# An encoder trunk on one core: the sample's laid-out x and one padded convolution row go to four buffers of their own

## The chip, the cores and the metric

The kernel runs on one core of a Trainium2 chip. The metric is device time in microseconds of one execution; each figure for the whole kernel is the median of several runs. All times inside the kernel are counted from the start of the span of one profiled execution.

The engines are called by their short names: PE (TensorE, matmuls), DVE (VectorE), ACT (ScalarE), POOL (GpSimd) and SP (SyncE, which here issues all DMAs). Each engine works through its own instructions strictly in order; an instruction that has to wait holds up all behind it on that engine.

## The reference

Two independent requests, a prompt of 512 tokens and a sample of 1024 tokens, go through one layer with the same weights (width 1024):

```
h = RMSNorm(x);  z = h @ w_in          # columns: q 512, k 128, v 128, ca 512, cb 512
A = windowed attention(q, k, v)         # 8 heads of 64, |q-k| <= 128, bias, sink
c = ca * sigmoid(cb)
B = silu(LayerNorm(depthwise_conv31(c)))
x = x + concat(A, B) @ w_out
u = depthwise_conv3(RMSNorm(x) @ w_up)
x = x + (silu(u[:, :2816]) * u[:, 2816:]) @ w_down
y = RMSNorm(x)
```

All is float32. A product is made of three matmuls: each operand is split into a rounded part "hi" and a remainder "lo", and hi*hi, hi*lo and lo*hi are summed.

## The kernel before, in words

**Stages.** The change concerns the first stage, the projection h @ w_in. The prompt's columns are made first, then the sample's, with the prompt's attention woven in. Channels lie on the partitions and 512 tokens along a row; the prompt is one such half (nt = 0), the sample two (nt = 1, 2).

**Weight chunks.** w_in is taken in chunks of 128 columns. `chunk_raw` (L222 to L225) loads one, 512 KB; `split` (L227 to L234) makes hi with an ACT copy (L230) and lo with a POOL subtraction (L231). Each of the three tiles is 4 KB a partition. `proj` (L347 to L350) then issues 24 matmuls for one chunk and one half.

**The order of the chunks** for the prompt is cb, ca of convolution rows 0, 1, 2, then k, v, then q 0 to 3, then cb, ca of row 3. `evac` brings each result out of PSUM. For "ca" it makes a padded convolution row (L427): 512 + 30 columns for the prompt, 1024 + 30 for the sample, with zeros at both ends by two POOL memsets (L428, L429) and the middle by DVE (L432). For "q" it makes hi and lo (L436, L437) and stores them in DRAM (L441, `qsd`), from where the attention loads them in another layout (L636).

**The convolution** (`conv_items`): 25 multiply-adds of DVE into one PSUM bank behind a first multiply (L398, L402), five further taps by ACT and POOL (L391, L394, L395) for the prompt, a sum (L410), and a store to DRAM (L412).

**The sample's h** (`make_h1`, `landed`). For each half, the host's transposed copy of x is loaded in four pieces of 4 KB a partition (`load_xT`, L496: the "laid-out x"). Four matmuls (L513) spread 1/rms over a PSUM bank; DVE scales each piece (L520, two for each piece), ACT rounds (L522), and DVE and POOL in turn subtract (L523). The next piece is loaded when the one ahead is taken up.

**Buffers.** `Slots.tile` hands out named buffers from free lists: of those that are large enough the smallest size, and of these the one free for longest. There are 15 "q" (4096 bytes a partition), 4 "c" (4224), 61 "h" (2048) and 2 "d" (2176). An optional `among` limits the choice to some kinds. A buffer that is handed out again brings a wait: its first writer waits for the last reader of what lay in it. So before the change the laid-out x and the weight chunks (raw, hi, lo) share the 15 "q"; the four "c" serve only the sample's four padded rows; the prompt's four padded rows lie in d0, d1, a "q" and d0 again.

**What sets the order.** In this stage a list scheduler with its own cost model lays out each engine's instructions when the program is built; with other buffers it finds other waits and makes another order. The same priorities and the same instructions go in. From the second feed-forward pass on, PE's order is written by hand.

**Names.** In the order below, a tile is named by its kind and two running numbers (b_39 is a PSUM bank's 39th use); where the buffer is shown, its number stands behind the letter (q7 is the eighth "q"). Bank uses: a_34, a_35, a_36, u_37 are the prompt's q 0 to 3; b_39 and b_40 are cb and ca of row 3; b_41 and b_48 are the sample's first chunk; u_42, a_43, a_44, a_45 are scores of the first attention unit and u_46 the first of the second unit. `h_169`, `h_174`, `h_179`, `h_185` are the lo tiles of q 0 to 3, `q_209` holds q as loaded for the first two units.

## Time and profile before

| | |
|---|---|
| median of 3 runs | 1494.17 us (1493.98 to 1497.1) |
| span of the profiled execution | 1495.0 us, 0.8 above that median; no other time of this execution is shown |
| PE busy | 1474.9 us, 99% of the span |
| DVE busy | 1142.9 us, 76% |
| ACT busy | 799.9 us, 54% |
| POOL busy | 676.3 us, 45% |
| mean granted PE clock | 0.997 of full speed |

A row of the timeline gives start, duration, engine, line, operation, output and inputs, and in brackets how long the engine had been idle and who released it. Matmuls overlap: a row of 0.39 us is followed by the next after 0.23 us. A row of the waits gives who waited for whom, the sum, the number of times and the longest. A row of the windows gives, for a stretch, the busy time of each engine, the granted PE clock, the busy share of the DMA engines and the GB/s.

### The profile page before, as it was taken

Reading aid. Unit: us, or ns where it says so; the run is one execution under the profiler, and the core shown is the slowest. Engines: PE = TensorE matmul, PEld = TensorE weight load, DVE = VectorE, ACT = ScalarE, POOL = GpSimd, SP = SyncE. Lnnn points to the kernel's source line nnn. Section 1 sums busy time; section 2 is a strip of 40 time slices with the busy share of each in tenths; the row PEclk is TensorE's granted clock in tenths of the full one; section 3 lists DMA queues with packets and bytes.
Section 4 is the critical chain, followed back from the end, with each engine's and each line's share of the span. In section 5 each row is a group of like instructions: output and inputs, shape, how many; then the busy total and the mean of one; then the engine's idle time right before and its main releaser. Section 6 shows DMA issues by size and latency. Waiting matters only on the chain.

```text
span 1495.0 us, 19855 instructions
## 1 busy us (share of the span) xinstructions
PE 1474.9 (99%) x6808; PEld 1222.4 (82%) x6808; DVE 1142.9 (76%) x1616; ACT 799.9 (54%) x1417; POOL 676.3 (45%) x540
## 2 busy tenths in 40 slices
PE   9989999999999999999999999999999999999998
PEld 7878888887888888778888888888887888888886
DVE  4999998778689876856868777777776855568884
ACT  7635665336777776444355555544444633434354
POOL 6842444235656565744325555555544000003345
PEclk9999999999999999999999999999999999999999
DMA  8862346274433346784213333333332772356644
GB/s 281 278 198 81 99 122 198 86 220 137 133 113 117 123 130 218 239 284 165 85 57 107 106 106 104 100 102 102 101 114 79 226 266 85 109 173 226 216 167 169
DMA packets 221761, 225.08 MB, mean 151 GB/s; under 512 B 12331, under 2 KB 161843, under 8 KB 221532
## 3 DMA queue, kind: packets, MB, share of 16 engines
q1 hardware_dynamic: 221660, 223.82, 46.5%
q8 instruction: 53, 0.87, 0.2%
q14 instruction: 48, 0.39, 0.1%
HBM read 164.77 MB, written 60.05 MB: 150 GB/s over the span
## 4 chain that ended last, share of the span: by engine, by line
PE 51%; DMA 3%; DVE 2%; POOL 2%; issue 1%; ACT 1%; SPq 0%; POOLq 0%; DVEq 0%; ACTq 0%
PE w L1227 9%; PE w L1228 9%; PE w L1229 9%; PE w L1578 7%; PE w L1577 7%; PE w L1579 7%; DMA c<-gt 2%; DMA gb<-c 1%; PE u L838 1%; PE u L840 1%; PE u L839 1%; DVE h L231 1%; DVE q L1090 0%; PE c L838 0%; PE c L839 0%
## 5 line engine op out<-in xcount | busy, mean ns | idle before, releaser
L231 POOL TENSOR_TENSOR q<-q,q 128x1024 fp32r<-128x1024 f32 x71 | 172.0, 2429 | 95.9 <-ACT q L230 28.2
L1090 POOL TENSOR_TENSOR q<-q,q 128x512 fp32r<-128x512 f32 x101 | 142.8, 1421 | 149.2 <-ACT q L1213 138.3
L1090 DVE TENSOR_TENSOR h<-h,h 128x512 fp32r<-128x512 f32 (+2 forms) x202 | 156.7, 809 | 64.9 <-ACT h L1094 27.3
L1579 PE MATMUL w<-h,h 128*128 128x512 f32 x462 | 179.7, 389 | 0.0
L1577 PE MATMUL w<-h,h 128*128 128x512 f32 x458 | 178.2, 389 | 0.0
L1578 PE MATMUL w<-h,h 128*128 128x512 f32 x458 | 178.2, 389 | 0.0
L1227 PE MATMUL w<-h,q 128*128 128x512 f32 x448 | 174.9, 390 | 1.4 <-ACT w L1310 1.1
L1229 PE MATMUL w<-h,q 128*128 128x512 f32 x448 | 174.3, 389 | 0.0
L1228 PE MATMUL w<-h,q 128*128 128x512 f32 x426 | 165.8, 389 | 0.0
L347 PE MATMUL u<-h,q 128*128 128x512 f32 x368 | 146.7, 399 | 2.5 <-DVE h L967 2.5
L348 PE MATMUL u<-h,q 128*128 128x512 f32 x368 | 144.4, 392 | 0.0
L350 PE MATMUL u<-h,q 128*128 128x512 f32 x360 | 141.4, 393 | 0.3
L402 DVE SCALAR_TENSOR_TENSOR c<-c,cvw,c 128x512 f32<-128x512 f32 x184 | 138.1, 751 | 2.5
L1087 POOL TENSOR_TENSOR q<-q,q 128x1024 f32<-128x1024 f32 x12 | 32.3, 2706 | 229.7 <-DMA h<-gb 190.0
L1094 ACT CAST h<-h 128x512 fp32r<-128x512 f32 x120 | 72.2, 622 | 97.6 <-DVE h L1090 41.5
L347 PE MATMUL b<-h,q 128*128 128x512 f32 x264 | 105.6, 400 | 4.8 <-ACT q L230 4.8
L348 PE MATMUL b<-h,q 128*128 128x512 f32 x264 | 104.3, 395 | 0.0
L350 PE MATMUL b<-h,q 128*128 128x512 f32 x264 | 103.9, 395 | 0.0
L1579 PEld LDWEIGHTS w<-h,h 128*128 128x128 f32 x462 | 86.7, 188 | 18.0
L1577 PEld LDWEIGHTS w<-h,h 128*128 128x128 f32 x458 | 86.0, 188 | 18.0
L1578 PEld LDWEIGHTS w<-h,h 128*128 128x128 f32 x458 | 86.0, 188 | 17.7
L1227 PEld LDWEIGHTS w<-h,q 128*128 128x128 f32 x448 | 84.1, 188 | 19.6 <-ACT w L1310 1.5
(447 smaller groups left out, 3649.9 us busy)
## 6 DMA issues: line engine op xcount, KB each, us to landing
q<-in_w_up SPq DMA_DIRECT2D x88, 512.0 KB, 4.4
ga<-q SPq DMA_DIRECT2D x64, 256.0 KB, 2.0
h<-ga SPq DMA_DIRECT2D x57, 256.0 KB, 3.3
q<-in_w_in SPq DMA_DIRECT2D x28, 512.0 KB, 4.6
h<-in_w_down SPq DMA_DIRECT2D x52, 256.0 KB, 3.5
q<-in_x_sample SPq DMA_DIRECT2D x15, 512.0 KB, 7.0
x1d<-q SPq DMA_DIRECT2D x11, 512.0 KB, 2.6
gt<-h SPq DMA_DIRECT2D x22, 256.0 KB, 2.4
```

The costliest lines, as they stand in the source:

```text
L231: ins = (nc.vector if dve else nc.gpsimd).tensor_tensor(lo[:], raw[:], hi[:].bitcast(F32), op=ALU.subtract)
L347: nc.tensor.matmul(out, whi[:, kc, :], hi[:], start=(kc == 0), stop=False)
L348: nc.tensor.matmul(out, whi[:, kc, :], lo[:], start=False, stop=False)
L350: nc.tensor.matmul(out, wlo[:, kc, :], hi[:], start=False, stop=(kc == KC - 1))
L402: nc.vector.scalar_tensor_tensor(acc[:], src(t), w(t), acc[:], op0=ALU.mult, op1=ALU.add)
L1090: (eng or nc.vector).tensor_tensor(out, a, b, op=ALU.subtract)
L1227: nc.tensor.matmul(out, whi[:, s], hi[:], start=(start and c == 0), stop=False, **go)
L1228: nc.tensor.matmul(out, whi[:, s], lo[:], start=False, stop=False, **go)
L1229: nc.tensor.matmul(out, wlo[:, s], hi[:], start=False, stop=(stop and c == 3), **go)
L1577: nc.tensor.matmul(out, sh[:, c], th[:], start=(p == 0), stop=False)
L1578: nc.tensor.matmul(out, sh[:, c], tl[:], start=False, stop=False)
L1579: nc.tensor.matmul(out, sl[:, c], th[:], start=False, stop=(p == NPAIR - 1))
```

## The change

Two buffers are chosen differently. The laid-out x (L495) takes a "c" buffer always. The padded row number 3 (L427) takes a "c" buffer; for the sample it did already, since nothing else is large enough, so this concerns the prompt's.

```diff
@@ evac, "ca", n == 0
-                cp = sb.tile([T + 2 * PAD])
+                cp = sb.tile([T + 2 * PAD], among="c" if c == 3 else None)
@@ load_xT
-            t = xT[nt, k] = sb.tile([2, NT])
+            t = xT[nt, k] = sb.tile([2, NT], among="c")
```

Eight pieces of x and five padded rows now go through the four "c" buffers, one behind another, and the 15 "q" are left to weight chunks, the rows of x for the norm, and smaller tiles. No instruction is added or removed. The orders move up to about the sample's convolutions. Three places follow.

**POOL, around the last subtraction of the laid-out x** (L523 is that subtraction, L231 the lo part of a chunk). Before:

```order
L231 TENSOR_TENSOR q10_156_845<-q1_136_763,q5_155_844 128x1024
L523 TENSOR_TENSOR h23_167_896<-q11_158_860,h57_166_895 128x512
L428 MEMSET d0_197_1138 128x15
L429 MEMSET d0_197_1138 128x15
L523 TENSOR_TENSOR h25_162_869<-q7_146_810,h54_161_868 128x512
L231 TENSOR_TENSOR q3_188_1055<-q1_180_1004,q4_187_1054 128x1024
L231 TENSOR_TENSOR q11_182_1007<-q9_175_959,q7_181_1006 128x1024
```

and with the change:

```order
L231 TENSOR_TENSOR q6_182_1007<-q10_175_959,q11_181_1006 128x1024
L231 TENSOR_TENSOR q13_188_1055<-q12_180_1004,q14_187_1054 128x1024
L523 TENSOR_TENSOR h21_144_797<-c0_135_756,h24_143_796 128x512
L231 TENSOR_TENSOR q2_195_1103<-q4_186_1052,q3_194_1102 128x1024
L523 TENSOR_TENSOR h34_153_839<-c1_139_777,h28_152_838 128x512
L523 TENSOR_TENSOR h25_162_869<-c2_146_810,h54_161_868 128x512
L523 TENSOR_TENSOR h23_167_896<-c3_158_860,h57_166_895 128x512
L231 TENSOR_TENSOR q10_208_1174<-q0_193_1100,q1_207_1173 128x1024
L428 MEMSET c0_197_1138 128x15
```

Before, the hi part of chunk 181 is written into q7, from which the subtraction h25_162 reads a piece of x; now it is written into q11, and the pieces lie in c0 to c3. The two last chunks of the prompt (181, 187) are split ahead of these subtractions, no longer behind.

**DVE, up to the lo part of the prompt's last q** (h_185, L437). Before:

```order
L402 SCALAR_TENSOR_TENSOR c_30_716<-d_76_518,cvw,c_30_716 128x512 x10
L437 SCALAR_TENSOR_TENSOR h_174_951<-a_35_921,h_173_950 128x512
L402 SCALAR_TENSOR_TENSOR c_30_716<-d_76_518,cvw,c_30_716 128x512
L437 SCALAR_TENSOR_TENSOR h_179_995<-a_36_965,h_178_994 128x512
L402 SCALAR_TENSOR_TENSOR c_30_716<-d_76_518,cvw,c_30_716 128x512
L437 SCALAR_TENSOR_TENSOR h_185_1043<-u_37_1010,h_184_1042 128x512
```

and with the change:

```order
L437 SCALAR_TENSOR_TENSOR h_169_906<-a_34_848,h_168_905 128x512
L402 SCALAR_TENSOR_TENSOR c_30_716<-d_76_518,cvw,c_30_716 128x512
L471 TENSOR_TENSOR h_150_830<-b_33_825,h_150_830 128x4x64
L523 TENSOR_TENSOR h_141_781<-c_135_756,h_140_780 128x512
L437 SCALAR_TENSOR_TENSOR h_174_951<-a_35_921,h_173_950 128x512
L523 TENSOR_TENSOR h_148_814<-c_139_777,h_147_813 128x512
L523 TENSOR_TENSOR h_160_864<-c_146_810,h_159_863 128x512
L523 TENSOR_TENSOR h_165_884<-c_158_860,h_164_883 128x512
L402 SCALAR_TENSOR_TENSOR c_30_716<-d_76_518,cvw,c_30_716 128x512
L471 TENSOR_TENSOR h_151_833<-b_33_825,h_151_833 128x4x64
L437 SCALAR_TENSOR_TENSOR h_179_995<-a_36_965,h_178_994 128x512
L437 SCALAR_TENSOR_TENSOR h_185_1043<-u_37_1010,h_184_1042 128x512
```

Fourteen L402 of the second convolution (c_30) now stand ahead of this piece, so 16 of them come before h_185 where it was 12; the 25 of the first (c_23) come before it in both. The second half's work on the laid-out x (L520, L523) now stands right in front of the lo parts of q; before it stood ahead of the second convolution.

**PE, around the first scores** (L672). Before, the first unit's scores stand within the sample's first chunk, b_41:

```order
L347 MATMUL b_41_1177<-h_105_638,q_194_1102 128x512
L348 MATMUL b_41_1177<-h_106_639,q_194_1102 128x512
L672 MATMUL u_42_1196<-h_128_735,q_209_1191 128x256
L672 MATMUL u_42_1196<-h_129_736,q_209_1191 128x256
L672 MATMUL a_43_1201<-h_128_735,q_209_1191 128x256
L672 MATMUL a_43_1201<-h_129_736,q_209_1191 128x256
L350 MATMUL b_41_1177<-h_105_638,q_195_1103 128x512
```

and with the change right behind b_39, ahead of all of b_41:

```order
L348 MATMUL b_39_1058<-h_38_291,q_181_1006 128x512
L350 MATMUL b_39_1058<-h_37_290,q_182_1007 128x512
L672 MATMUL u_42_1196<-h_128_735,q_209_1191 128x256
L672 MATMUL u_42_1196<-h_129_736,q_209_1191 128x256
L672 MATMUL a_43_1201<-h_128_735,q_209_1191 128x256
L672 MATMUL a_43_1201<-h_129_736,q_209_1191 128x256
L672 MATMUL a_44_1212<-h_128_735,q_209_1191 128x256
```

Before, 17 matmuls of b_41 precede u_42 and all 24 precede u_46; now none do, and they follow. Also, b_40 now comes as a whole ahead of b_39, and before b_39 came first by two matmuls.

## The prediction

> **What bounds the kernel now.** I read the page first. PE is busy for 99% of the span, so only its waits can be won, and they are listed by the view of waits for PE.

> ```profile
> span 1495.0 us, 19855 instructions
> PE 1474.9 (99%) x6808; PEld 1222.4 (82%) x6808; DVE 1142.9 (76%) x1616; ACT 799.9 (54%) x1417; POOL 676.3 (45%) x540
> PE b L347 <- ACT q L230: 4.8, 1, 4.8
> ```

> The longest wait is the one that touches this change: PE waits once for the hi part of a weight chunk. The timelines of PE, ACT, POOL and SP at that place show why.

> ```profile
> 83.03 0.39 PE L350 MATMUL a<-h,q 128*128 128x512 f32 x1
> 83.72 0.39 PE L350 MATMUL a<-h,q 128*128 128x512 f32 x1
> 88.94 0.80 PE L347 MATMUL b<-h,q 128*128 128x512 f32 x1 [4.84 <-ACT q L230]
> 92.44 0.40 PE L347 MATMUL b<-h,q 128*128 128x512 f32 x1
> 84.46 1.05 ACT L230 CAST q<-q 128x1024 fp32r<-128x1024 f32 x1 [5.10 <-DMA q<-in_w_in]
> 87.84 1.99 ACT L230 CAST q<-q 128x1024 fp32r<-128x1024 f32 x2 [2.34 <-POOL h L523]
> 86.54 1.27 POOL L523 TENSOR_TENSOR h<-q,h 128x512 fp32r<-128x512 f32 x1 [4.84 <-DMA cvd<-h]
> 82.24 0.34 SPq L412 DMA_DIRECT2D cvd<-h  x1
> 90.00:92.00 2.00, 2.00 (x6) 1.61 (x5) 1.97 (x4) 1.75 (x3) 2.00 (x2) 0.50 0.15 39
> ```

> PE stops after 83.72 and goes on at 88.94, when the second cast of ACT ends. That cast (chunk 181) writes q7, which L523 on POOL reads until 87.8; and this L523 waited 4.84 us for the store of the first convolution, which was issued at 82.24 and whose source it overwrites. Behind the wait PE runs at half the granted clock (0.50): from 88.94 to 92.44 are eight steps in 3.50 us. At full clock three steps take 83.72 - 83.03 = 0.69, so 0.23 each and 1.82 for eight. The stall costs 4.84 + 1.68 = **6.5 us**.

> But PE is not alone at its limit here. Grouped by shape from 25 to 95 us, and in the timeline, DVE shows:

> ```profile
> 45.00:60.00 15.00, 15.00 (x72) 12.57 (x71) 14.89 (x17) 11.80 (x21) 14.68 (x15) 1.00 1.05 362
> 60.00:75.00 15.00, 14.90 (x68) 12.01 (x67) 14.93 (x16) 7.83 (x13) 11.66 (x7) 1.00 0.53 141
> L402 DVE SCALAR_TENSOR_TENSOR c<-d,cvw,c 128x512 f32<-128x512 f32 x39 | 29.3, 752 | 0.8
> L523 DVE TENSOR_TENSOR h<-q,h 128x512 fp32r<-128x512 f32 x8 | 16.1, 2026 | 0.0
> L447 DVE TENSOR_TENSOR h<-u,h 128x512 fp32r<-128x512 f32 x1 | 0.7, 684 | 0.0
> 25.75 0.17 DVE L578 COPY vecs<-c 128x12 f32<-128x12 f32 x1 [7.22 <-PE c L570]
> 32.19 0.68 DVE L595 COPY h<-c 8x512 f32<-8x512 f32 x1 [4.70 <-PE c L593]
> 93.47 0.69 DVE L437 SCALAR_TENSOR_TENSOR h<-u,h 128x512 fp32r<-128x512 f32 x1
> ```

> In the windows the fourth number with a count is DVE's: 14.89 and 14.93 of 15 us. From 25.75 to the end of h_185 (93.47 + 0.69 = 94.16) DVE idles 4.70 us before L595 and twice 0.2, and works for 68.4 - 5.1 = 63.3 us. The eight L523 take 2.03 us each, although a subtraction of the same size takes 0.68 (L447): they meet POOL's work.

> **The change, part by part.** *The removed wait.* Chunk 181's hi now goes to q11, the last readers of which do not include an L523, and its cast stands far ahead. So the wait of 4.84 us and its half-clock phase go: -6.5. L523 of POOL may still wait for a convolution's store, but nothing of PE stands behind it.

> *The first half's x.* Its four loads move ahead of the chunk loads: 4 x 512 KB. DMA has room for them soon after: the stretch

> ```profile
> 28.00:33.00 5.00, 5.00 (x21) 3.18 (x20) 0.78 (x2) 5.00 (x8) 5.00 (x3) 1.00 0.22 71
> 33.00:45.00 12.00, 12.00 (x56) 9.90 (x55) 11.42 (x17) 6.31 (x12) 11.68 (x11) 1.00 0.97 344
> ```

> has DMA at 0.22, and at the 344 GB/s of the next row 2.1 MB take 6.1 us. Chunk loads come that much later, but the first of them is wanted by PE only behind the whole of b_24, at about 32.7. I charge nothing; without that cover the price is one load's 1.5 us. DVE fills its 4.70 us of idle time with the eight L520.

> *POOL's early order.* Between the first L395 (27.9) and the lo part of chunk 81 now stand 4 L395, 3 L231 and 3 L523. By the groups of POOL

> ```profile
> L231 POOL TENSOR_TENSOR q<-q,q 128x1024 fp32r<-128x1024 f32 x14 | 34.2, 2464 | 0.7 <-ACT q L230 0.7
> L523 POOL TENSOR_TENSOR h<-q,h 128x512 fp32r<-128x512 f32 x8 | 12.2, 1520 | 7.5 <-DMA cvd<-h 4.8 <-ACT h L522 2.7
> L395 POOL TENSOR_TENSOR h<-h,h 128x512 f32<-128x512 f32 x8 | 10.8, 1350 | 0.2
> ```

> that is 5.4 + 7.4 + 4.6 = 17.4, so 45.3. PE, with two more matmuls in front, wants it at 44.4: a new wait of 0.9 us. It costs nothing as long as PE waits longer for DVE later (next part); alone it costs the 0.9.

> *DVE's order, the step that decides.* The idle time is filled, but four more L402 come before h_185 (41, not 37): 25.75 + 63.3 + 4 x 0.75 = **92.1**, only 2.1 us earlier than 94.2. Behind h_185 hang its store, the load of q_209 for the second unit, and u_46. Before, this ran:

> ```profile
> 90.36 6.61 SPq L441 DMA_DIRECT2D qsd<-h  x10
> 99.36 0.58 SPq L636 DMA_DIRECT2D q<-qsd  x1
> 100.04 0.84 SPq L621 DMA_DIRECT2D h<-bbd  x2
> 100.93 0.90 SPq L636 DMA_DIRECT2D q<-qsd  x2
> DMA to landing us min/median/max: 5.1/5.1/5.1
> DMA to landing us min/median/max: 2.8/2.8/2.8
> 105.38 0.40 PE L672 MATMUL u<-h,q 128*128 128x256 f32 x2
> 107.94 0.40 PE L672 MATMUL u<-h,q 128*128 128x256 f32 x2
> ```

> The two landing times are of the load at 100.93 and of a lone one at 135. With the change: SP takes 0.66 us a store and issues those of h_179 and h_185 from 91.5 to 94.1, then two L621 (0.42 each), the first unit's q_209 at 95.0 and, when the last store has landed (2.4 us, as the stores of the two other stretches), the second unit's at 96.5. Two chunk loads of 512 KB no longer stand between, so the landing lies between 2.8 and 5.1; I take the middle, 4.0. First scores at 99.0, u_46 at **100.5**.

> PE is there earlier. It now runs through 83.95, needs b_40 (24 x 0.23 = 5.5) and is ready for b_39 at 89.5; b_39's bank is freed by the L471 two L437 before the end of h_185, at 90.7: wait 1.2. b_39 ends at 96.2; wait 2.8 for the first scores; these take 1.0; wait 0.5. Sum of new waits **4.5**, and by the row

> ```profile
> 658.96 0.79 PE L839 MATMUL u<-h,h 128*128 128x512 f32 x1 [2.00 <-DVE h L231]
> 659.00:662.00 3.00, 3.00 (x7) 2.42 (x8) 2.52 (x4) 1.19 (x2) 1.02 (x2) 0.50 0.82 337
> 349.00:352.00 3.00, 3.00 (x14) 2.45 (x14) 2.90 (x6) 1.72 (x3) 3.00 (x3) 1.00 0.41 121
> 348.52 0.47 PE L347 MATMUL u<-h,q 128*128 128x512 f32 x1 [1.55 <-DVE h L967]
> ```

> a wait of 2.00 us brought half clock, one of 1.55 us not. With 3.3 us of 4.3 idle I expect the half clock; part of it falls on the short score matmuls, so I charge 1.2 of the 1.68. Sum: -6.5 + 4.5 + 1.2 = -0.8, rounded down to **-0.7 us**. As a check, from the other side: u_46 and then b_41 end at 100.5 + 0.2 + 5.5 = 106.2, with 1.2 at 107.4; before, the same work ended at 108.2.

> [...]

> *Later parts.* The sample's last padded row (c0) now waits for the last read of the prompt's fourth convolution. Its memset on POOL has an L707 and an L231 behind it; before, POOL idled 7.45 us and 4.70 us near there, which covers a few us.

> ```profile
> 166.42 2.41 POOL L231 TENSOR_TENSOR q<-q,q 128x1024 fp32r<-128x1024 f32 x1 [4.70 <-ACT s L699]
> 181.21 2.39 POOL L231 TENSOR_TENSOR q<-q,q 128x1024 fp32r<-128x1024 f32 x1 [7.45 <-ACT q L230]
> ```

> **The rivals.** *One: the full gain.* If the L523 no longer meet POOL's work as often, DVE gets ahead of PE. It needs 4.5 us, 0.56 for each of the eight: a mean of 1.47 instead of 2.03. At 0.68 it would be 10.8. For it: POOL's work is split up otherwise. Against: POOL is as full as before in both stretches, and the second four L523 of DVE now stand beside four L523 and two L231 of POOL. Time 1494.2 - 6.5 = 1487.7, or 1488.6 with the early wait of 0.9.

> *Two: slower.* The same term the other way. PE now has nothing in front of u_42 and u_46, where before 24 matmuls (5.5 us) covered the way over DRAM. If h_185 ends later than about 93, each further us is paid in full. At the longest L523 that the trace has,

> ```profile
> L523 DVE TENSOR_TENSOR h<-q,h x8: 1290/2001/2820, 44.8 to 75.7; 128x512 fp32r<-128x512 f32 x8
> ```

> 2.82 for all eight, the end comes 6.4 later: 1494.2 + 5.7 = 1499.9; at 2.5, 1497.3. For it: the order is a scheduler's, which put u_42 there for data that it believed to be ready. Against: the mean was 2.03 with POOL just as busy.

> *Three: no half clock.* The idle time comes as three waits with work between them, of which the first and the last (1.2 and 0.5) are shorter than the 1.55 us at 348.52, behind which the clock stayed at 1.00; only the middle one (2.8) is longer than the 2.00 at 658.96. If the work between them keeps the clock up, 1.2 us fall away: 1492.3. Against it is the row at 659, where PE had work on both sides too. [...]

> *Four: nothing moves at the wait,* because another late reader holds the buffer of chunk 181: 1494. Against it is the order, in which the cast stands ahead.

> **How the numbers follow.** Measured against its own execution the change brings -0.7 to a span of 1495.0; the median is 0.8 below that span, so I take 1494.2 - 0.7 = **1493.5**. Chances: forecast 0.47, full gain 0.24, slower 0.16, no half clock 0.10, nothing 0.03. A landing of 2.8 or 5.1 moves the forecast by 1.2, to 1492.3 or 1494.6. The range of 8 in 10 reaches towards both sides: down to 1488.0 (between the two times of the full gain, about half of which it leaves out) and up to 1497.0 (L523 at nearly 2.5). About 0.2% (3.0 us) is what a measurement can tell from no change. Faster by more is nearly all of the full gain and a little of the third rival, 0.25; slower by more 0.15 of the 0.16; the rest, 0.60, within.

> **What would show it.** Right: no PE wait for L230 at 84 us; L437 of h_185 ending at 91 to 93; PE waiting for DVE at b_39 and for a load at L672, 3 to 6 us in all, and half clock behind it; eight L523 of about 2.0 us. Wrong: L523 means near 1.4 or 2.6, no wait at L672, or new waits of PE between 110 and 350 us, where there are none now up to 348.5.

## The result and the profile after

The changed kernel took 1498.94 us (median of 15 runs, 1495.48 to 1504.42) against 1495.33 us of the kernel before (15 runs): ratio **1.0020, 95% interval 1.0010 to 1.0029**. The ratio on record is not that of the two medians, which lie 3.6 us apart; by the ratio the change is 3.0 us slower (1.5 to 4.3), where 0.7 us faster was forecast. The predicted range ended at 1497.0. In every run an execution's time is its span plus 1.8 us, so the execution whose span of 1495.0 the prediction started from had taken 1496.8 us, 1.5 above the median of all runs of before, and not 0.8.

PE's waits in the changed kernel, from the view of waits, and the same places in PE's timeline (the row at 95.89 is the last matmul of b_39):

```profile
span 1498.9 us, 19853 instructions
PE u L672 <- DMA q<-qsd: 3.4, 1, 3.4
PE u L672 <- DVE s L679: 1.9, 1, 1.9
PE a L350 <- POOL q L231: 1.4, 1, 1.4
46.08 0.50 PE L350 MATMUL a<-h,q 128*128 128x512 f32 x1 [1.37 <-POOL q L231]
95.89 0.39 PE L350 MATMUL b<-h,q 128*128 128x512 f32 x1
99.68 0.50 PE L672 MATMUL u<-h,q 128*128 128x256 f32 x2 [3.41 <-DMA q<-qsd]
102.81 0.77 PE L672 MATMUL u<-h,q 128*128 128x256 f32 x2 [1.91 <-DVE s L679]
```

The wait of 4.84 us at 84 us is gone. In its place are 1.37 us at 46, then, behind the last matmul of b_39, 3.41 us in front of the first score (u_42) and 1.91 us in front of the second unit's (u_46): 6.7 us instead of 4.8. The windows of this stretch show the half clock behind them; the number in front of the DMA share is the granted clock.

```profile
100.00:102.00 2.00, 0.90 (x8) 0.69 (x6) 0.05 (x1) 0.00 (x0) 0.00 (x0) 0.77 0.83 221
102.00:104.00 2.00, 1.19 (x4) 1.12 (x5) 2.00 (x8) 1.21 (x5) 0.00 (x0) 0.50 0.98 367
...
106.00:108.00 2.00, 2.00 (x6) 1.58 (x5) 1.61 (x3) 0.57 (x1) 1.28 (x1) 0.52 0.01 4
```

A window of 2 us at 0.77 holds 2 x 0.23 / 0.5 = 0.92 us of half clock, one at 0.52 holds 1.92; with the two full ones between, the phase lasts 6.84 us, twice the 3.4 of before. By PE's busy time in each window it costs 2.8 us, where before it was 1.4.

Why the scores waited stands in the timelines of DVE, ACT, POOL and SP, in a group of DVE from 25 to 95 us, in SP's own waits, and in the list of DMA issues from 93 to 105 us:

```profile
60.85 0.69 DVE L447 TENSOR_TENSOR h<-u,h 128x512 fp32r<-128x512 f32 x1 [2.12 <-ACT h L446]
89.80 0.68 DVE L437 SCALAR_TENSOR_TENSOR h<-u,h 128x512 fp32r<-128x512 f32 x1
L523 DVE TENSOR_TENSOR h<-c,h 128x512 fp32r<-128x512 f32 x8 | 11.5, 1462 | 0.0
92.17 1.95 ACT L394 ACTIVATE h<-q,cvw 128x512 f32<-128x512 f32 x3 [6.14 <-DMA qsd<-h]
92.97 2.68 POOL L395 TENSOR_TENSOR h<-h,h 128x512 f32<-128x512 f32 x2 [2.05 <-ACT h L394]
94.31 1.72 SPq L621 DMA_DIRECT2D h<-bbd  x2
96.11 0.38 SPq L636 DMA_DIRECT2D q<-qsd  x1
97.06 0.38 SPq L636 DMA_DIRECT2D q<-qsd  x1
SPq L621 <- POOL h L395: 2.3, 2, 1.4
q<-qsd SPq DMA_DIRECT2D x3, 256.0 KB, 5.7
```

DVE was not late: h_185 ended at 90.48. But on SP two loads of the bias (L621) stand in front of the first load of q. Their buffers are those of two taps of the convolution (h55 and h26 in the order), so each waits for the L395 that reads the tap; the first L395 waits for L394 on ACT, and that one for the stores of q, in whose buffers the taps are written. So the first load of q went out at 96.11, the second at 97.06. The first score followed the first load by 3.5 us. The second unit's score came at 102.81, which is the second load's issue plus 5.7, the median landing of these loads: 102.8. The row names L679, the last thing that DVE had finished; but u_46 reads nothing of L679, and its bank (u0) was last read by the L437 that ended at 90.48. In two more profiles of this order the sum fits as well (below).

### The profile page after: what moved, and what is told of

The parts are those of the page before. It is cut to its first block, busy times and chain, and to the rows that moved or that the text cites. A ratio compares the mean times of both kernels' runs of the same rounds, so it can differ in the third digit from the quotient of the medians.

```text
span 1498.9 us, 19853 instructions
## 1 busy us (share of the span) xinstructions
PE 1477.1 (99%) x6808; PEld 1223.7 (82%) x6808; DVE 1136.3 (76%) x1616; ACT 796.7 (53%) x1417; POOL 676.1 (45%) x540
## 4 chain that ended last, share of the span: by engine, by line
PE 91%; DMA 3%; DVE 2%; POOL 1%; ACT 1%; issue 1%; SPq 0%; POOLq 0%; DVEq 0%; ACTq 0%
PE w L1227 9%; PE w L1228 9%; PE w L1229 9%; PE w L1578 7%; PE w L1579 7%; PE w L1577 7%; PE u L347 5%; PE u L348 5%; PE u L350 5%; PE b L348 3%; PE b L350 3%; PE b L347 3%; PE u L839 2%; PE u L838 2%; PE u L840 2%; PE a L672 1%
## 5 line engine op out<-in xcount | busy, mean ns | idle before, releaser
L231 POOL TENSOR_TENSOR q<-q,q 128x1024 fp32r<-128x1024 f32 x71 | 172.2, 2428 | 95.5 <-ACT q L230 23.1
L1227 PE MATMUL w<-h,q 128*128 128x512 f32 x448 | 174.9, 390 | 1.1 <-ACT w L1310 0.8
L402 DVE SCALAR_TENSOR_TENSOR c<-c,cvw,c 128x512 f32<-128x512 f32 x209 | 156.8, 750 | 2.9
L347 PE MATMUL u<-h,q 128*128 128x512 f32 x368 | 147.1, 400 | 2.8 <-DVE h L967 2.8
L350 PE MATMUL u<-h,q 128*128 128x512 f32 x360 | 141.9, 394 | 0.1
L347 PE MATMUL b<-h,q 128*128 128x512 f32 x264 | 105.5, 400 | 0.0
L350 PE MATMUL b<-h,q 128*128 128x512 f32 x264 | 104.4, 395 | 0.0
L1227 PEld LDWEIGHTS w<-h,q 128*128 128x128 f32 x448 | 84.1, 188 | 19.4 <-ACT w L1310 1.2
```

The lines of the kernel that those rows point to most:

```text
L231: ins = (nc.vector if dve else nc.gpsimd).tensor_tensor(lo[:], raw[:], hi[:].bitcast(F32), op=ALU.subtract)
L347: nc.tensor.matmul(out, whi[:, kc, :], hi[:], start=(kc == 0), stop=False)
L350: nc.tensor.matmul(out, wlo[:, kc, :], hi[:], start=False, stop=(kc == KC - 1))
L402: nc.vector.scalar_tensor_tensor(acc[:], src(t), w(t), acc[:], op0=ALU.mult, op1=ALU.add)
L1227: nc.tensor.matmul(out, whi[:, s], hi[:], start=(start and c == 0), stop=False, **go)
```

## Experiments

Each kernel was timed beside before, in one series of runs. The table gives, for the one profiled execution of each, PE's waits and its loss by half clock (sum over windows of 2 us of PE's busy time times one minus the clock) from 20 to 130 us and from 330 us to the first L1227, and the time of that instruction, all in us. Behind them stand, over all runs, the median, the median of before in the same series, and the ratio on record with its interval.

| kernel | 20 to 130: waits, half | 330 on: waits, half | first L1227 | median | before | ratio |
|---|---|---|---|---|---|---|
| before | 4.8, 1.4 | 4.8, 1.5 | 729.37 | | | |
| the change | 6.7, 2.8 | 4.6, 3.3 | 733.41 | 1498.94 | 1495.33 | 1.0020 (1.0010 to 1.0029) |
| the change again | 6.8, 4.0 | 4.0, 1.5 | 732.44 | 1499.15 | 1497.13 | 1.0016 (1.0005 to 1.0028) |
| x only | 5.6, 3.1 | 4.7, 0.0 | 730.04 | 1499.48 | 1495.47 | 1.0022 (1.0013 to 1.0031) |
| row only | 3.7, 2.8 | 5.1, 1.6 | 729.81 | 1497.17 | 1495.47 | 1.0004 (0.9993 to 1.0015) |
| scores behind | 3.2, 0.0 | 5.8, 1.7 | 728.04 | 1495.45 | 1495.47 | 1.0001 (0.9988 to 1.0013) |
| q first | 2.8, 0.0 | 5.4, 0.0 | 725.43 | 1496.27 | 1495.47 | 1.0002 (0.9992 to 1.0012) |
| first half's x | 4.5, 1.5 | 4.3, 0.0 | 727.05 | 1494.75 | 1496.14 | 0.9991 (0.9981 to 1.0001) |
| second half's x | 4.4, 0.0 | 4.8, 0.0 | 727.52 | 1495.64 | 1496.14 | 0.9992 (0.9983 to 1.0001) |
| q first, scores behind | 2.8, 0.0 | 6.2, 0.0 | 727.49 | 1495.13 | 1496.14 | 0.9993 (0.9983 to 1.0002) |
| bias early, scores behind | 16.1, 2.3 | 4.6, 0.0 | 741.33 | 1508.45 | 1496.14 | 1.0072 (1.0059 to 1.0084) |
| lo first | 3.8, 1.6 | 4.2, 1.7 | 727.48 | 1496.05 | 1497.13 | 0.9999 (0.9987 to 1.0011) |
| q and lo first | 3.1, 0.0 | 5.0, 1.7 | 726.13 | 1494.98 | 1497.13 | 0.9993 (0.9981 to 1.0005) |
| all three | 2.0, 0.0 | 5.1, 1.5 | 725.94 | 1493.13 | 1497.13 | **0.9980 (0.9968 to 0.9991)** |

From 130 to 330 us no kernel waits more than 0.9 us. The first L1227 less these four columns is 716.0 to 718.5 in every row: waits and half clock account for the differences to within 2.5 us.

The expectations were written when I still read the second wait as one for L679; where they say so, the load of q stands behind it.

### Which half of the change brings it

Only the x (the row as before), and only the row (the x as before):

```diff
-                cp = sb.tile([T + 2 * PAD], among="c" if c == 3 else None)
+                cp = sb.tile([T + 2 * PAD])
```
```diff
-            t = xT[nt, k] = sb.tile([2, NT], among="c")
+            t = xT[nt, k] = sb.tile([2, NT])
```

> Only the laid-out x takes c buffers; the prompt's fourth padded row stays where it was. Theory A (the loss comes from the first scores, which stand in front of the sample's first chunk b_41 with nothing to cover their loads; that order already comes with x alone): the old wait of 4.84 us at 84 us is gone, PE waits about 3.4 us for the load of q_209 and about 1.9 us for L679 near 96 to 103 us, and the time is 2 to 4 us above before. Rival D (the padded row, whose memsets and readers now stand in line in the c buffers, brings the loss): without the row the gain of the removed wait shows, 4 to 6 us below before.

> Only the prompt's fourth padded row takes a c buffer; the laid-out x stays among the q buffers. Theory A: the order on PE stays that of before (17 matmuls of b_41 ahead of the first scores), the wait of 4.84 us at 84 us stays, the time is that of before within 1.5 us. Rival D (the row brings the loss): 3 us or more above before, with new PE waits that before does not have.

PE's timeline with x only, then with the row only:

```profile
99.24 0.51 PE L672 MATMUL u<-h,q 128*128 128x256 f32 x2 [2.68 <-DMA q<-qsd]
102.03 0.77 PE L672 MATMUL u<-h,q 128*128 128x256 f32 x2 [1.58 <-DVE s L679]
```
```profile
87.94 0.79 PE L347 MATMUL b<-h,q 128*128 128x512 f32 x1 [3.72 <-ACT q L230]
```

x alone gives the change's order on PE and SP, its two waits and its loss; the row alone leaves the old wait and no difference that can be told. The loss is x's, and rival D is out. (With x only the second load went out at 97.22; plus its 4.7 that is 101.9, and the score came at 102.03.)

### What the place of the scores costs, and what the queue

The scores of the first four units are held behind the projection matmul that was written last before them:

```diff
+            if not late_lo:
+                ended["mm"] = ins.ins
...
-                nc.tensor.matmul(sc[:, :nk], ...)
+                with (tc.issue_after(ended["mm"]) if u < 4 and L == 0 else nullcontext()):
+                    nc.tensor.matmul(sc[:, :nk], ...)
```

or the loads of q are written ahead of those of the bias (the first ones then take h buffers):

```diff
-    load_bias()
 ...
+    load_q(0)
+    load_q(1)
+    load_bias()
```

> The change as it is, but the matmuls of the first four attention units (L672) may not be placed ahead of the projection matmul that stood last in the program when they were written: 12 matmuls of b_41 come before the first score, 24 before the second unit's. All loads, buffers and the order of the queue stay the same. Theory A (missing cover on PE makes the loss): PE reaches the first score at about 98.8 us instead of 96.05, waits at most 1 us for q_209 and not at all at the second unit, and stays at full clock: 4.4 us of waits and about 2.3 us of half clock less than the change, so about 3.5 us below before (1490 to 1493 for a before of 1495.3). Rival C (the loss lies in later parts, where the DVE or the convolutions have become late, and the waits at 96 to 103 us are only where it shows): the waits come back behind b_41 or later, and the time stays within 1.5 us of the change, 2 to 4 us above before.

> The change as it is, but in the program the loads of q for the first two units stand ahead of the eight loads of the bias (L621), so the queue has one bias load in front of them and not two or three, and they take other buffers. PE's order keeps the first scores ahead of b_41. Theory A, with the queue as what sets the length of the waits: the first score starts about 1.3 us earlier (98.4 us instead of 99.7), and the bias of the first head is there earlier, so that the wait of 1.9 us for L679 goes nearly; about 3 us below the change, that is the time of before within 1.5 us. Rival B (the lo parts of q on DVE and their stores set the start of the scores, as the prediction had it): the first score does not start earlier than 99.2 us and the time stays that of the change, 2 to 4 us above before.

PE with the scores behind, in which the lines have moved by two or three (L425 is L423, L730 is L727, L708 is L705); then SP, PE and DVE with q first (L634 is L636, L674 is L672, L681 is L679):

```profile
97.41 0.50 PE L347 MATMUL b<-h,q 128*128 128x512 f32 x1 [0.69 <-ACT h L425]
115.38 0.33 PE L730 MATMUL a<-ident,q 128*128 128x128 f32 x1 [1.19 <-ACT q L708]
```
```profile
94.85 1.32 SPq L634 DMA_DIRECT2D h<-qsd  x3
97.76 0.48 PE L674 MATMUL u<-h,h 128*128 128x256 f32 x2 [1.20 <-DMA h<-qsd]
98.79 0.40 PE L674 MATMUL u<-h,h 128*128 128x256 f32 x2
99.14 0.47 DVE L681 CUSTOM_DVE_ANT_0 q<-u,h,nsink 128x256 f32<-128x256 f32 x1
346.99 0.47 PE L347 MATMUL u<-h,q 128*128 128x512 f32 x1 [3.02 <-DVE h L969]
```

Each alone takes the loss back to before, so the two together made it: scores with nothing in front of them, and loads of q behind loads of the bias. Rival B, by which the first score would not start ahead of 99.2 us, is out (97.76). With the scores behind, b_41 runs from 97.41, where in the change it stood behind the waiting scores until 103.38, and the waits at the scores are gone; those that stay are for the bank of b_41, which tanh (L423) reads, and for the exponentials. With q first the three loads go out together at 94.85, the first score starts 1.9 us earlier than in the change and the second unit's (98.79) does not wait at all. It runs before the first L679 begins (99.14): so u_46 does not need L679, and its wait in the change was one for the load.

Theory A expected the scores-behind kernel at 1490 to 1493; it came at 1495.45. The stretch up to 130 us gave what was expected (9.5 us of waits and half clock in the change, 3.2 now), but only about half of it is in the time (ratios of 1.0020 and 1.0001: some 2.8 us, each known to between 1.5 and 2). One place where it goes back shows with q first: PE comes to the L967 wait at 346.99 - 3.02 = 343.97, 3.0 us earlier than before (348.52 - 1.55 = 346.97), and DVE releases it only 1.5 us earlier.

### Half of x

Only the first half's pieces, or only the second half's, in c (`among="c" if nt == 1 else None`, and `nt == 2`; the row as before).

> Only the first half's four pieces of x take c buffers; the second half's and the padded row stay as before the change. The list scheduler then puts the first scores still further forward: ahead of 22 matmuls of b_39 and of all of b_41. Theory A (the place of the scores on PE against the arrival of q sets the loss): PE comes to the first score some 5 us earlier than in the change and waits that much longer, 6 to 9 us in all, so the time is 4 us or more above the change (1503 or more). Rival E (the loss is that of eight pieces and five rows queueing for four buffers, which is half as much here): no slower than the change, 1495 to 1499.

> Only the second half's four pieces of x take c buffers. The old wait goes (the cast of chunk 181 waits for no L523), and the scheduler leaves 12 matmuls of b_41 in front of the first score and 24 in front of the second unit's. Theory A: without the uncovered loads the gain of the removed wait stays: no PE wait for L230 at 84 us, none above 1 us at the first scores, 3 to 6 us below before (1489 to 1492 for a before of 1495.3). Rival C (whatever is gained at 84 us is given back in later waits, since the sample's attention and convolutions are late by DVE and POOL): within 1.5 us of before, with new waits between 105 and 260 us.

SP and PE with the first half's; then PE with the second half's:

```profile
88.64 0.47 SPq L636 DMA_DIRECT2D q<-qsd  x1
84.50 0.71 PE L350 MATMUL a<-h,q 128*128 128x512 f32 x1 [2.42 <-POOL q L231]
96.65 0.40 PE L672 MATMUL u<-h,q 128*128 128x256 f32 x2
```
```profile
91.77 0.50 PE L350 MATMUL b<-h,q 128*128 128x512 f32 x1 [0.98 <-POOL q L231]
99.05 0.50 PE L347 MATMUL b<-h,q 128*128 128x512 f32 x1 [2.00 <-ACT h L423]
```

The first of these is a clear miss of theory A as I had put it. The scores stand ahead of b_39, and yet the first one does not wait: in this order the first load of q stands ahead of all bias loads, and went out at 88.64. The place on PE is not a loss by itself; only against the load's place in the queue. The second half's x alone keeps 12 matmuls of b_41 in front of the scores and has no half clock, but new waits of 0.98 and 2.00 us; it gives little.

### Both edits together, and the bias early

> The change with both edits of the two runs before: q's loads ahead of the bias loads in the program, and the first four units' scores kept behind the projection matmuls that stand ahead of them in the program. Theory A: no wait of PE at the first scores at all; what the run with the scores behind still had (0.7 us for L423 and 1.2 us for the exponentials) stays or shrinks; PE stands 5 us or more ahead of before at 250 us, and the time is 2 to 5 us below before. Rival C: the two do not add up, the time stays within 1.5 us of before like each alone, and the profile shows which later wait takes the gain.

> The change with the scores kept behind as above, and with the eight bias tiles loaded four chunks earlier in the program, so that no bias load stands in front of the first loads of q and no softmax (L679) waits for one. Theory A: no wait of PE for q or for L679 near 96 to 103 us, 2 to 5 us below before. Rival F (the bias tiles then hold buffers, one q, one d and six h, that the prompt's weight chunks and lo parts want, so new waits come before 96 us): a new PE wait between 60 and 96 us, and the time at or above that of before.

The second of these loads the eight bias tiles four chunks earlier, in the loop over the prompt's chunks:

```diff
     for i in range(npr):
+        if i == npr - 4:
+            load_bias()
```

PE with both edits (L972 is L967 there, L844 is L839); then ACT and PE with the bias early (L438 is L436, L425 is L423):

```profile
347.69 0.47 PE L347 MATMUL u<-h,q 128*128 128x512 f32 x1 [2.47 <-DVE h L972]
658.26 0.50 PE L844 MATMUL u<-h,h 128*128 128x512 f32 x1 [2.63 <-DVE h L231]
```
```profile
102.94 0.60 ACT L438 ACTIVATE h<-u 128x512 fp32r<-128x512 f32 x1 [5.25 <-DMA cvd<-h]
111.54 0.79 PE L347 MATMUL b<-h,q 128*128 128x512 f32 x1 [14.75 <-ACT h L425]
```

The two edits do not add up (0.9993), as rival C had it: no wait at the first scores is left, but the waits from 330 us on are 6.2 us. The early bias fails by rival F's mechanism, later than it said: with the bias in their buffers, the hi part of the prompt's last q has to go where the second convolution's sum lies until its store has landed, and everything behind it on ACT, tanh for the bank of b_41 among it, comes 14.75 us too late for PE.

### The early wait at 46 us

POOL's subtractions of the first half's x are held behind the chunk's lo part:

```diff
+            with (tc.issue_after(ended["pool"]) if kc % 2 and nt == 1 else nullcontext()):
                 (nc.gpsimd if kc % 2 else nc.vector).tensor_tensor(lo[:], t, hi[:].bitcast(F32), op=ALU.subtract)
```

alone, with q first, and with q first and the scores behind; and the change itself once more.

> The change, with POOL's subtractions of the first half's x (L523) kept behind the lo part of the weight chunk that stands last ahead of them in the program. The lo part of chunk 82 then comes before all four, and the queue happens to be laid out with the first unit's q load ahead of the stores of h_185 and of all bias loads. Theory A (the waits are set by where the load of q stands in the queue, and by the bias of head 0): the wait of 1.4 us at 46 us goes, the first score waits less than 1.5 us, the second unit's wait for L679 stays at 1 to 3 us, and the time is 2 to 4 us below the change, about that of before. The prediction's claim (an early wait costs nothing while a later one is longer): if the first score still waits until 99.2 us or later, the time is that of the change.

> The change with two edits: POOL's subtractions behind the chunk's lo part as in the run beside it, and q's loads ahead of the bias loads in the program. Theory A: neither the wait of 1.4 us at 46 us nor waits at the first scores above 2 us in all; by the sum of waits and of half clock up to 130 us (6.2 us of waits and half clock in before from 20 us on, at most 2 here) 3 to 4 us below before. Theory G (part of what PE wins early is waited for again at L967 near 347 us, where DVE is later than PE: with q's loads first alone PE came 3.0 us earlier and waited 1.5 us longer): 1 to 2.5 us below before, and a wait of 2.5 to 4 us at L967.

> The change with three edits: POOL's subtractions behind the chunk's lo part, q's loads ahead of the bias loads, and the scores kept behind the projection matmuls that stand ahead of them in the program. Theory A: the waits up to 130 us fall to about 1.5 us from 20 us on, 3 to 5 us below before. Theory G as in the run beside it: half of that, 1 to 2.5 us below before, with the wait at L967 grown to 2.5 to 4 us.

> The change itself once more, beside the three edits of it and beside before. All theories: 2 to 5 us above before; waits of 1.4 us at 46 us, 2.5 to 3.5 us for q and 1.5 to 2 us for L679 as in the first profile. Whether the waits of 1 to 3 us at L967 and L839 bring half clock may differ from the first profile, in which both did; if it does, the half clock behind such a wait is a matter of chance and explains a spread of some 1.6 us a time between executions of one kernel.

SP and PE with lo first (L637 is L636, L673 is L672); PE with all three edits (L473 is L471, L425 is L423, L973 is L967); SP and PE of the change again, with the first and the last window of its half clock:

```profile
87.70 0.46 SPq L637 DMA_DIRECT2D q<-qsd  x1
90.83 0.47 PE L347 MATMUL b<-h,q 128*128 128x512 f32 x1 [1.59 <-DVE h L471]
99.66 0.68 PE L673 MATMUL u<-h,q 128*128 128x256 f32 x2 [2.19 <-DVE h L410]
```
```profile
90.26 0.47 PE L347 MATMUL b<-h,q 128*128 128x512 f32 x1 [1.03 <-DVE h L473]
96.64 0.50 PE L347 MATMUL b<-h,q 128*128 128x512 f32 x1 [0.69 <-ACT h L425]
345.62 0.76 PE L347 MATMUL u<-h,q 128*128 128x512 f32 x1 [2.34 <-DVE h L973]
```
```profile
98.50 0.38 SPq L636 DMA_DIRECT2D q<-qsd  x1
100.76 0.79 PE L672 MATMUL u<-h,q 128*128 128x256 f32 x2 [4.26 <-DMA q<-qsd]
103.97 0.77 PE L672 MATMUL u<-h,q 128*128 128x256 f32 x2 [1.13 <-DVE s L679]
q<-qsd SPq DMA_DIRECT2D x3, 256.0 KB, 5.4
98.00:100.00 2.00, 0.00 (x0) 0.00 (x0) 1.89 (x4) 0.00 (x0) 1.39 (x1) 0.89 0.87 251
...
108.00:110.00 2.00, 2.00 (x7) 1.57 (x6) 0.76 (x1) 0.00 (x0) 1.92 (x2) 0.55 0.05 8
```

With lo first the wait at 46 us goes, and a wait of 1.59 us for L471 comes at b_39: the early wait had covered it. The first load of q goes out at 87.70 and the first score waits for nothing; u_46 waits 2.19, and here the row names L410, a sum of the convolution that no score reads, which again is no more than DVE's last event. All three edits leave 2.0 us of waits and no half clock up to 130 us and are **faster than before by 0.20% (0.09 to 0.32%)**, the best version found: x can go to its own buffers with a gain, if the three things that come with it are undone. The three edits were not run without the change, so how much of the gain they would bring by themselves is not shown. Of q and lo first, 0.9993, it can't be told whether theory A or G holds. The change again is slower than before again; its second load went out at 98.50, plus 5.4 is 103.9, and the score came at 103.97.

## Why the prediction was wrong

**The removed wait:** right, it went with its half clock, 6.2 us in before's profile where 6.5 were charged.

**The first half's x and the DMA:** right, no wait of PE for a chunk's load came. **Later parts:** right, PE waits nowhere between 110 and 330 us.

**POOL's early order:** right in place and kind (PE at 46.08 waits for the lo part), 1.37 us instead of 0.9. That it costs nothing as long as a later wait is longer was right too: the wait at b_39 for L471, forecast at 1.2 us, did not come in the change, and came (1.59, 0.96, 1.03 us) in the three kernels without the early wait.

**DVE's order, "the step that decides":** this step failed. h_185 ended at 90.48, not 92.1: the eight L523 took 1.46 us in the mean, 4.5 us less in all, and DVE gave 2.1 of that back before L447 at 60.85. That L523 takes longer beside POOL's work, as the prediction has it, can't be read from L447's 0.68, since L447 ran beside POOL too. Another subtraction of that size in before shows it, L231 on DVE: 0.69 us at 241.90, with POOL idle, and 1.78 at 251.05, with POOL busy throughout; but one L523 of the change, at 82.49, took 0.68 beside POOL. A mean below 1.47 is the condition of the rival *full gain*, and the gain did not come, because DVE was not what came last. The loads of q stood on SP behind two loads of the bias, and these behind POOL's taps. I had listed both L621 in front with their 0.42 us each and had not asked what their buffers wait for. It made the first issue 96.11 instead of 95.0 and the second 97.06 instead of 96.5.

**The landing:** mis-sized. The middle of 2.8 and 5.1 was 4.0; the first load took about 3.5, within the bounds, and the second 5.7, above both. Seven more loads of bias and q were sent out from 94.31 to 98.9, and the DMA share was 0.98 at 102 to 104 us; that these made the second load late is likely and not tested by itself. So the first score came at 99.68 instead of 99.0, and u_46 at 102.81 instead of 100.5. That I expected u_46 to wait for the second load was right.

**The half clock:** mis-sized. It cost 2.8 us, and 1.2 were charged.

With these terms the sum closes: waits 6.7 instead of 4.5 (the early wait in the place of that at b_39) are +2.2, the half clock +1.6; -0.7 + 3.8 = +3.1 us, and 3.0 were measured. That it fits so well is partly luck: the terms are of one execution, the 3.0 is of all runs and known to about 1.4, and in the two profiles the first L1227 came 4.0 us later.

**The rivals.** *Slower* came true in its direction and in its reason that nothing stands in front of u_42 and u_46; what was late was not h_185. Its time (1497.3 to 1499.9) holds 1498.94, but before's median was 1495.33 here and not 1494.2; against before, 3.0 us is just short of its smallest loss, 3.1. *No half clock* is out: the clock fell in all three profiles of this order. *Nothing moves* is out.

**What is open.** Why the edits' gain up to 130 us comes through so unevenly: against before, all three edits save 4.2 us there and bring 3.0, q first saves 3.4 and brings nothing. In part these columns are not typical of their kernels: the profiled execution of q first took 1493.34 us, 2.9 below its median, and that of before 1496.8, 1.5 above; from the one to the other the gain is 3.5. That DVE's releases near 347 us come later than PE is shown for one of them (q first); the waits from 330 us on are 4.0 to 6.2 us in all kernels, with no order that would explain it.

## What to carry to other kernels

When a change of buffers lets a scheduler move work, price the moved consumer by the whole way of its data: not only the producer, but every instruction ahead of the load in its queue, and what the buffer of each of these waits for. Work that stood in front of a consumer by chance is cover; look what fills the gap before you count a removed wait as gained. Where a row names an engine for a wait on several things, test it by adding the load's landing to its issue.

## What the runs showed of the hardware that was not expected

**The half clock came in whole pieces of 3.4 us.** It lasted 1.08 + 2 + 0.32 = 3.4 us in before (windows from 88 to 94, whose clocks are 0.73, 0.50 and 0.92), 6.84 in the change, 17.04 from 99.12 with the bias early, and 0.44 + 4 x 2 + 1.8 = 10.24 in the change again, which is three times 3.413. Where PE worked all through it, a piece cost 1.7 us, half its length.

```profile
88.00:90.00 2.00, 1.06 (x3) 0.87 (x4) 1.93 (x3) 2.00 (x3) 2.00 (x1) 0.73 0.05 14
...
92.00:94.00 2.00, 2.00 (x9) 1.62 (x8) 2.00 (x4) 0.00 (x0) 2.00 (x2) 0.92 0.77 195
```

**Whether a wait of about 2 us brought it depended on where it fell.** Over the 14 profiles, and counting waits with no other of over 1 us within 8 us, none of some 40 waits of PE from 0.8 to 1.8 us was followed by half clock. Of 22 from 1.8 to 3.1 us, 11 were, from 1.81 up, and 11 were not, up to 3.02 (the wait at 346.99 with q first). The same wait of the same order differed between executions: L967 near 352 us brought it after 2.76 us in the change, and not after 2.79 us with x only. Windows of 3.41 us, the length of a piece, laid from the falls and rises of the clock in the same profile, show a difference; first the change, then x only.

```profile
350.26:353.67 3.41, 0.99 (x4) 0.86 (x5) 2.86 (x5) 1.88 (x4) 3.41 (x3) 1.00 0.55 158
353.67:357.08 3.41, 3.41 (x10) 2.63 (x9) 3.38 (x8) 1.47 (x2) 3.41 (x2) 0.50 0.02 5
347.10:350.51 3.41, 2.17 (x10) 1.47 (x8) 0.67 (x1) 2.50 (x4) 3.27 (x2) 1.00 0.55 166
350.51:353.92 3.41, 1.87 (x8) 1.60 (x9) 3.07 (x6) 1.88 (x4) 3.41 (x2) 1.00 0.55 158
```

A piece is 1.7 us, and the 15 runs of before spread over 6.5 us; such pieces are a part of that spread (in the 15 runs of the change the mean granted clock lies between 0.993 and 0.998, and the slowest run, 1504.42, has the lowest).
